# Sixteen column-block sums of a decoder layer's first modulation, in another order and at other places of VectorE's program

## The chip, the cores and the metric

The kernel runs on one core of a Trainium2 chip. The metric is the time of one execution on the device, in microseconds (us). The core has five engines that run their own programs and wait for each other through semaphores: TensorE (PE in the profile, with its weight loads as PEld), VectorE (DVE), ScalarE (ACT), GpSimd (POOL) and SyncE (SP), which here issues most of the transfers from memory.

## The reference

One decoder layer on a sequence of 1024 tokens of width 1024, in float32. A conditioning vector `c` gives six rows of 1024 numbers, the modulation; the first two, shift and scale of the token-mixing part, are what this change deals with. Cut to that:

```python
mod = c_act @ w_ada[l] + b_ada[l]          # c_act = silu(c), w_ada: 1024 x 6144
sh1, sc1, g1, sh2, sc2, g2 = [m[:, None, :] for m in jnp.split(mod, N_MOD, axis=-1)]
h = rmsnorm(x, pre_w_mix[l]) * (1.0 + sc1) + sh1
proj = h @ w_in[l]                         # attention q, k, v and the recurrence's inputs
...
mix = jnp.concatenate([attn, rec], axis=-1) @ w_out[l]
x = x + g1 * rmsnorm(mix, post_w_mix[l])
h = rmsnorm(x, pre_w_mlp[l]) * (1.0 + sc2) + sh2
u = jnp.square(jax.nn.relu(h @ w_up[l]))
x = x + g2 * rmsnorm(u @ w_down[l], post_w_mlp[l])
```

## The kernel before

The program is one long function that lays the layer out in stages: the first modulation together with the first projections (about the first 70 us), attention, the gated recurrence, the output projection, and the channel mixing, which is half of the time. All matrix products are done in split precision: each operand is a rounded part `h` (hi) and a rest `l` (lo), and three products hi x hi, hi x lo, lo x hi are summed.

**The first stage.** Tokens go in groups of four blocks of 128; the width of 1024 goes in eight column blocks `kb` of 128. The loop over `kb` (lines 430 to 485) does for the first 512 tokens:

- `first_evac`: the transposed tokens of block `kb`, `xT` in PSUM, are scaled and shifted by the modulation. ScalarE writes the hi part `hhi`, POOL forms `f` from it, VectorE writes the rest `hlo` from `xT` and `f`.
- `first_mm(kb, tb, 0)`: TensorE multiplies `hhi` by the weights `wq` and `wkv`, hi and lo. These matmuls are `pq` and `pk` in the profile.
- `first_wql`, `first_kv`: VectorE makes the lo parts of the next weights (`wq1l` and so on).
- `first_T`: TensorE transposes the tokens of the next block. There is one PSUM buffer for `xT`, so this waits until `hlo` of the block before has been written.
- `first_mm(kb, tb, 1)`: TensorE multiplies `hlo` by the hi weights.

Shift and scale of a block must be there before its `first_evac`. The modulation's columns are made in four parts, `q`. For the first two parts (columns blocks 0 to 3 of `kb`) TensorE sums over the 1024 inputs itself (`mod_mm`, `mod_copy`, `mod_fold`; tiles `pm` and `ms`). For the last two, `(2, 0)` and `(3, 0)`, VectorE does: `mod_sum` takes eight weight tiles of 128 x 512, multiplies each by a column of `cs` and adds it to `macc1`; `mod_turn` has TensorE transpose the sum (`pmt`), VectorE reduces it (`mred`) and four short operations make the shift `sh1` and the scale `a1`. Part `(2, 0)` serves the column blocks 4 and 5, part `(3, 0)` the blocks 6 and 7, so `mod_turn` stands at the ends of `kb` 3 and 5.

**The weight tiles.** `load_wa` loads them from memory, part by part, and within a part in the order `kp` 0 to 3 with `gate` 0 and 1 in turn (lines 353 to 356). `mod_sum`'s index `k` means tile `wa1[q, k % 4, k // 4]`, that is `kp = k % 4` and `gate = k // 4`. So the tiles are loaded in the order k = 0, 4, 1, 5, 2, 6, 3, 7. In the program order below, `wa1_20_3` is gate 1 of part 2 with kp 3, hence k = 7; the last number of a name is a buffer number.

**What sets the order.** The order is written out by hand. Line 360 pins ScalarE, VectorE, POOL and TensorE: from there on each engine runs its instructions in the order in which the code issues them, and an instruction that waits holds back all behind it on its engine. The sync queue issues its loads in the order of the code too.

**The places the change touches** are the calls of `mod_sum`: at line 469, behind `mod_fold` and `mod_turn` of `kb` 2 and 4, for k = 0 to 4, and at line 461, at the head of the second half of `kb` 3 and 5, for k = 5 to 7:

```python
        if kb in (3, 5):
            mod_sum((kb // 2 + 1, 0), range(5, KB))
...
        if kb in (2, 4):
            mod_sum((kb // 2 + 1, 0), range(5))
```

Of the kernel before, what the change touches and what calls it, by code (L numbers as in the profile page):

```python
# [18 lines left out]
KB = D // P  # L19
# [28 lines left out]
def hybrid_layer(ctx: ExitStack, tc: tile.TileContext, I, out, dbg=None):  # L48
# [3 lines left out]
    def pin(on, *engines):  # L52
        for e in engines:
            e.pinned = on
# [31 lines left out]
    def t_(name, shape=(P, 512), dt=F32):  # L86
        return T2.tile(list(shape), dt, tag="t2", name=name)
# [4 lines left out]
    def tp_ps(name):  # L92
        return pb.tile([P, 512], F32, tag="b", name=name)

    def a_ps(name):
        return pa.tile([P, 512], F32, tag="aps", name=name)
# [8 lines left out]
    def load_x(tb, hfs=(0, 1)):  # L105
        for hf in hfs:
            xh[tb][hf] = (m_ if tb < 4 else hT_)(f"x{tb}_{hf}")
            SP.dma_start(xh[tb][hf], I["x"][tb * P:(tb + 1) * P, hf * 512:(hf + 1) * 512])
# [99 lines left out]
    def norm_scale(th, hf, eng, tbs=range(4)):  # L208
        for tb in tbs:
            xt = xh[4 * th + tb][hf]  # L210
            if eng is ACT:
                ACT.activation(xt, xt, AF.Copy, scale=rx[th][:, tb:tb + 1])
            else:
                DVE.tensor_scalar(xt, xt, rx[th][:, tb:tb + 1], None, ALU.mult)

    def first_T(th, kb, mk=tp_ps):
        pst = mk(f"xT{th}_{kb}")
        hf, col = kb // 4, (kb % 4) * P
        for j in range(4):
            PE.transpose(pst[:, j * P:(j + 1) * P], xh[th * 4 + j][hf][:, col:col + P], ident)  # L220
        return pst
# [12 lines left out]
    def first_evac(th, kb, pst, then=None):  # L234
        hh[kb][th] = (hT_(f"hhi{kb}_{th}", F32R), hT_(f"hlo{kb}_{th}", F32R))
        c = slice(kb, kb + 1)
        split_evac(pst, a1[:, c], sh1[:, c], ns1[:, c], *hh[kb][th], f"f{th}_{kb}", then)
# [4 lines left out]
    def load_raw(mk, name, src, eng=None):  # L242
        rw = mk(name)
        (eng or SP).dma_start(rw, src)
        return rw

    def load_split(mk, name, src, eng=None, raw=None):
        hi, lo = mk(name + "h", dt=F32R), mk(name + "l", dt=F32R)
        for c in range(0, src.shape[1], 512):
            rw = load_raw(raw_, f"{name}r{c}", src[:, c:c + 512]) if raw is None else raw  # L250
            hc = hi[:, c:c + 512]
            ACT.activation(hc, rw, AF.Copy)
            (eng or DVE).tensor_tensor(lo[:, c:c + 512], rw, hc.bitcast(F32), ALU.subtract)
        return hi, lo
# [26 lines left out]
    def mod_mm(q, kps=range(4)):  # L281

        n = 256 if q[0] else P
        if kps[0] == 0:
            pm[q] = a_ps(f"pm{q[0]}_{q[1]}")
        for kp in kps:
            for i in range(4):
                w2 = wa1[q, kp, i // 2][:, i % 2 * 256:][:, :256] if q[0] else wa1[q, kp, 0][:, P * i:P * i + P]
                PE.matmul(pm[q][32 * i:32 * i + 32, :n], lhsT=csr[:, 2 * kp + i % 2, :], rhs=w2,
                          start=(kp == 0), stop=(kp == 3), tile_position=(0, 32 * i))  # L290

    def mod_copy(q):
        n = 256 if q[0] else P
        pm[q, 0] = t_(f"ms{q[0]}_{q[1]}", (P, n))
        DVE.tensor_copy(pm[q, 0], pm[q][:, :n])
# [16 lines left out]
    def mod_sum(q, ks):  # L312
        for k in ks:
            wt, c = wa1[q, k % 4, k // 4], cs[:, k:k + 1]
            if k == 0:
                macc1[q] = t_(f"macc1_{q[0]}")
                DVE.tensor_scalar(macc1[q], wt, c, None, ALU.mult)
            else:
                DVE.scalar_tensor_tensor(macc1[q], wt, c, macc1[q], ALU.mult, ALU.add)
# [82 lines left out]
    def first_kv(qt, eng=POOL):  # L402
        hi, lo = load_split(m_, f"wkv{qt}", I["w_kv"][qt], eng=eng, raw=wkvr[qt])
        wkv.extend([(hi[:, 0:256], lo[:, 0:256]), (hi[:, 256:512], lo[:, 256:512])])
# [13 lines left out]
    def first_wq(kb):  # L418
        hi, lo = (g_(f"wq{kb}{n}", dt=F32R) for n in "hl")
        ACT.activation(hi, wqr[kb], AF.Copy)  # L420
        wq.append((hi, lo))

    def first_wql(kb):
        hi, lo = wq[kb]
        DVE.tensor_tensor(lo, wqr[kb], hi.bitcast(F32), ALU.subtract)
# [4 lines left out]
    for kb in range(KB):  # L430
        q = nextq.get(kb)
        first_evac(0, kb, xT0[kb], None if kb else lambda: first_kv(0, DVE))
        if kb == 0:
            pq0 += [tp_ps("pq2"), tp_ps("pq3")]
            pks = [tp_ps("pk01"), tp_ps("pk23")]
            pk0 += [pks[tb // 2][:, tb % 2 * 256:tb % 2 * 256 + 256] for tb in range(4)]
            wkvr.append(load_raw(raw_, "wkvr3", I["w_kv"][3]))
        if kb + 1 < KB:
            first_wq(kb + 1)
        if kb == 3:  # L440
            norm_scale(0, 1, ACT)
            pin(True, SP)
            for hf in range(2):
                for tb in range(4, TB):
                    load_x(tb, (hf,))
            pin(False, SP)
        if kb and q:
            mod_mm(q, range(2))
        for which in ((0,), (1,)) if kb == 0 else ((0, 1),):
            first_mm(kb, 0, 0, which)  # L450
            first_mm(kb, 1, 0, which)
            if kb and q:
                mod_mm(q, range(2, 4))
                mod_copy(q)
            first_mm(kb, 2, 0, which)
            first_mm(kb, 3, 0, which)
            if kb == 0 and which[0] == 0:
                mod_mm(q)
                mod_copy(q)
        if kb in (3, 5):  # L460
            mod_sum((kb // 2 + 1, 0), range(5, KB))
        if kb + 1 < KB:
            first_wql(kb + 1)
        if q:
            mod_fold(q)
        if kb in (3, 5):
            mod_turn((kb // 2 + 1, 0))
        if kb in (2, 4):
            mod_sum((kb // 2 + 1, 0), range(5))
        if kb in (1, 3, 5):  # L470
            first_kv((kb + 1) // 2, DVE)
        if kb + 1 < KB:
            xT0.append(first_T(0, kb + 1))
        if kb in (5, 6):
            for tb in range(4, TB):
                norm_sq(tb, (kb - 5,))
        if kb == 6:
            norm_rstd(1, 0, 4)
            norm_scale(1, 0, DVE)
        if kb == 7:  # L480
            norm_scale(1, 1, DVE)
        if kb == KB - 1:
            xT1 = [first_T(1, 0), first_T(1, 1, a_ps)]
        for tb in range(4):
            first_mm(kb, tb, 1)
# [1290 lines left out]
```

## Time and profile before

| | before |
|---|---|
| median of 3 runs | 1097.88 us (1097.61 to 1098.4) |
| the profiled execution, as a run | 1101.11 us |
| its span, first to last instruction | 1099.3 us |
| instructions | 16110 |
| moved between memory and the core | 203.37 MB, 185 GB/s in the mean |

The profile is of one execution. A busy time is the time in which an engine executed something, a share is that of the span. Rows of a timeline give start and duration in us, the engine, the line, the operation, the tile written, the tiles read, the sizes and the count; in brackets stands the idle time ahead and what ended it. All operations of a pinned engine go through a helper and so carry one line, L39: they are told apart by their tiles. Names are cut there to their letters, so `macc1_2` and `macc1_3` are both `macc`, the two `mod_turn` both `pmt`.

The busy share of VectorE in the 40 slices of the span (27.5 us each, in tenths), with that of TensorE above it, shows where the first stage lies, in the first two to three slices:

```profile
PE   8999999999999999999999999999999999999995
...
DVE  3875777878865574559767767676678787999876
```

### The profile page before, as it was taken

Reading aid. Unit: us, or ns where it says so; the run is one execution under the profiler, and the core shown is the slowest. Engines: PE = TensorE matmul, PEld = TensorE weight load, DVE = VectorE, ACT = ScalarE, POOL = GpSimd, SP = SyncE. Lnnn points to the kernel's source line nnn. Section 1 sums busy time; section 2 is a strip of 40 time slices with the busy share of each in tenths; the row PEclk is TensorE's granted clock in tenths of the full one; section 3 lists DMA queues with packets and bytes.
Section 4 is the critical chain, followed back from the end, with each engine's and each line's share of the span. In section 5 each row is a group of like instructions: output and inputs, shape, how many; then the busy total and the mean of one; then the engine's idle time right before and its main releaser. Section 6 shows DMA issues by size and latency. Waiting matters only on the chain.

```text
span 1099.3 us, 16110 instructions
## 1 busy us (share of the span) xinstructions
PE 1074.6 (98%) x5483; PEld 877.0 (80%) x5483; DVE 802.8 (73%) x1339; ACT 583.6 (53%) x1206; POOL 373.1 (34%) x499
## 2 busy tenths in 40 slices
PE   8999999999999999999999999999999999999995
PEld 6788776788888888888888888888878888888884
DVE  3875777878865574559767767676678787999876
ACT  3445544364565764566655555556575543446434
POOL 1153211043324653432543443434233333330014
PEclk9999999999999999999999999999999999999998
DMA  9701301534310352324577676767799888998637
GB/s 350 257 11 52 122 1 38 185 103 140 124 57 13 105 183 96 125 79 143 191 249 249 229 259 203 260 218 255 267 376 318 274 291 259 341 311 271 187 80 131
DMA packets 101586, 203.37 MB, mean 185 GB/s; under 512 B 13024, under 2 KB 13680, under 8 KB 101504
## 3 DMA queue, kind: packets, MB, share of 16 engines
q1 hardware_dynamic: 85968, 154.52, 41.6%
q0 software_dynamic: 15392, 47.57, 14.6%
q8 instruction: 43, 0.70, 0.3%
q14 instruction: 39, 0.32, 0.1%
q10 hardware_dynamic: 144, 0.26, 0.1%
HBM read 147.25 MB, written 55.05 MB: 184 GB/s over the span
## 4 chain that ended last, share of the span: by engine, by line
PE 83%; DMA 7%; DVE 5%; ACT 2%; issue 1%; POOL 1%; SPq 0%; DVEq 0%; POOLq 0%; ACTq 0%
PE pda L39 14%; PE pua L39 13%; PE pdc L39 7%; PE po L39 7%; PE puc L39 6%; PE pu L39 4%; PE pdb L39 4%; PE phg L39 4%; PE phq L39 3%; PE phf L39 3%; PE pub L39 3%; PE pv L39 3%; PE pq L39 2%; DMA wa<-wada 1%; DMA dwr<-td 1%
## 5 line engine op out<-in xcount | busy, mean ns | idle before, releaser
L39 POOL TENSOR_TENSOR b<-b,b 128x512 f32<-128x512 f32 x64 | 88.8, 1388 | 235.5 <-DMA b<-w_dn 235.2
L39 ACT ACTIVATE dw<-dwr 128x512 fp32r<-128x512 f32 x72 | 45.4, 630 | 48.3 <-DMA dwr<-td 30.9
L39 ACT ACTIVATE s<-s 128x512 f32<-128x512 f32 x84 | 52.9, 631 | 33.3 <-DVE s L39 32.0
L39 DVE TENSOR_TENSOR acc<-pda,acc 128x512 f32<-128x512 f32 x68 | 46.9, 689 | 15.3 <-PE pda L39 14.9
L39 DVE TENSOR_TENSOR dw<-dwr,dw 128x512 fp32r<-128x512 f32 x72 | 53.6, 744 | 5.8 <-ACT dw L39 5.8
L39 POOL DMA_DIRECT2D td<-b x64 | 36.3, 567 | 21.6 <-POOL b L39 18.7
L39 ACT ACTIVATE s<-pua 128x512 f32<-128x512 f32 x28 | 16.7, 597 | 39.5 <-PE pua L39 34.0
L39 ACT ACT_TABLE_LOAD x28 | 35.9, 1283 | 1.2 <-PEq L1769 0.7
L39 POOL TENSOR_TENSOR rrf<-ssf,mhalf 128x1 f32<-128x1 f32 x7 | 7.8, 1252 | 83.9 <-DVE ssf L39 83.9
L39 DVE TENSOR_TENSOR wt<-s,wt 128x512 fp32r<-128x512 f32 x42 | 33.8, 805 | 2.6 <-ACT wt L39 2.5
L39 DVE SCALAR_TENSOR_TENSOR macc<-wada,cs,macc 128x512 f32<-128x512 f32 x42 | 33.4, 795 | 3.0 <-DMA wada<-wada 2.5
L39 POOL DMA_DIRECT2D b<-w_dn x64 | 34.4, 540 | 0.0
L39 POOL TENSOR_TENSOR comb<-comb,rd 128x512 f32<-128x512 f32 x8 | 11.7, 1458 | 63.3 <-DVE rd L39 44.2
L39 PE MATMUL pua<-bt_0h,wt 128*128 128x512 f32 x84 | 32.7, 389 | 0.0
L39 PE MATMUL pua<-bt_1h,wt 128*128 128x512 f32 x84 | 32.7, 389 | 0.0
L39 PE MATMUL pua<-bt_2h,wt 128*128 128x512 f32 x84 | 32.7, 389 | 0.0
L39 PE MATMUL pua<-bt_3h,wt 128*128 128x512 f32 x84 | 32.7, 389 | 0.0
L39 DVE TENSOR_TENSOR wt<-a,wt 128x512 fp32r<-128x512 f32 x42 | 31.6, 753 | 0.9 <-ACT wt L39 0.9
L39 ACT ACTIVATE wt<-s 128x512 fp32r<-128x512 f32 x42 | 26.3, 626 | 8.9 <-DVE s L39 8.7
L39 DVE TENSOR_TENSOR s<-puc,s 128x512 f32<-128x512 f32 x14 | 9.7, 690 | 28.5 <-issue 26.0
L39 PE MATMUL pda<-dw,du_6h 128*128 128x512 f32 x96 | 29.8, 390 | 0.5 <-DVE dw L39 0.5
L39 DVE TENSOR_TENSOR acc<-pdc,acc 128x512 f32<-128x512 f32 x36 | 24.8, 690 | 7.3 <-PE pdc L39 7.1
(763 smaller groups left out, 3775.4 us busy)
## 6 DMA issues: line engine op xcount, KB each, us to landing
dur<-ud SPq DMA_DIRECT2D x112, 256.0 KB, 4.7
wada<-wada SPq DMA_DIRECT2D x64, 256.0 KB, 3.8
b<-w_dn POOLq DMA_DIRECT2D x64, 256.0 KB, 5.4
td<-b POOLq DMA_DIRECT2D x64, 256.0 KB, 3.5
dwr<-td SPq DMA_DIRECT2D x64, 256.0 KB, 4.4
a<-w_u SPq DMA_DIRECT2D x56, 256.0 KB, 4.3
dwr<-w_dn SPq DMA_DIRECT2D x48, 256.0 KB, 4.8
ud<-s SPq DMA_DIRECT2D x42, 256.0 KB, 3.6
```

The costliest lines, as they stand in the source:

```text
L39: ins = op(*args, **kw)
```

## The change

The sixteen calls of `mod_sum` for single tiles are taken in the order in which the tiles are loaded and set at other places of the loop. Within each part the set of tiles is the same; only the order of the additions and the places differ.

```diff
@@ -451,24 +451,33 @@
             if kb and q:
                 mod_mm(q, range(2, 4))
+                mod_sum((2, 0), (0, 4))
                 mod_copy(q)
...
-        if kb in (3, 5):
-            mod_sum((kb // 2 + 1, 0), range(5, KB))
         if kb + 1 < KB:
             first_wql(kb + 1)
+        if kb == 1:
+            mod_sum((2, 0), (1,))
+        if kb == 3:
+            mod_sum((3, 0), (0,))
         if q:
             mod_fold(q)
         if kb in (3, 5):
             mod_turn((kb // 2 + 1, 0))
-        if kb in (2, 4):
-            mod_sum((kb // 2 + 1, 0), range(5))
+        if kb == 2:
+            mod_sum((2, 0), (2, 6, 3, 7))
+        if kb == 4:
+            mod_sum((3, 0), (5, 2, 6, 3, 7))
         if kb in (1, 3, 5):
             first_kv((kb + 1) // 2, DVE)
+        if kb == 1:
+            mod_sum((2, 0), (5,))
+        if kb == 3:
+            mod_sum((3, 0), (4, 1))
```

What that does to VectorE's program, at three places. Each row is one instruction: the line, the operation, the tile written, the tiles read, the size.

**In `kb` 1.** Before, between the rest `hlo1` and the shift and scale of the blocks 2 and 3 (`m1s1`), VectorE's program has the copy of TensorE's partial sums and one weight's lo part:

```order
L39 SCALAR_TENSOR_TENSOR hlo1_0_410<-xT0_1_396,a1_130,f0_1_412 128x512
L39 COPY ms1_0_443<-pm1_0_418 128x256
L39 TENSOR_TENSOR wq2l_416<-wqr2_181,wq2h_415 128x512
L39 TENSOR_TENSOR m1s1_0_456<-pm1_0_418,c_tab_97 128x2
L39 TENSOR_TENSOR sh1_128<-pm1_0_418,c_tab_97 128x2
```

The same place in the changed program:

```order
L39 SCALAR_TENSOR_TENSOR hlo1_0_410<-xT0_1_396,a1_130,f0_1_412 128x512
L39 TENSOR_SCALAR macc1_2_443<-wa0_20_0_187,cs_107 128x512
L39 SCALAR_TENSOR_TENSOR macc1_2_443<-wa1_20_0_189,cs_107,macc1_2_443 128x512
L39 COPY ms1_0_446<-pm1_0_418 128x256
L39 TENSOR_TENSOR wq2l_416<-wqr2_181,wq2h_415 128x512
L39 SCALAR_TENSOR_TENSOR macc1_2_443<-wa0_20_1_191,cs_107,macc1_2_443 128x512
L39 TENSOR_TENSOR m1s1_0_460<-pm1_0_418,c_tab_97 128x2
```

Three sums of the part for the blocks 4 and 5 (k = 0, 4, 1) now stand here, two ahead of the copy and one behind the lo part; the fourth (k = 5) stands a few rows on, ahead of `hlo2`.

**In `kb` 2 and 3.** Before, from the lo part `wq3l` to `mred`, the first operation behind the transposes of the finished sum:

```order
L39 TENSOR_TENSOR wq3l_485<-wqr3_183,wq3h_484 128x512
L39 TENSOR_SCALAR macc1_2_504<-wa0_20_0_187,cs_107 128x512
L39 SCALAR_TENSOR_TENSOR macc1_2_504<-wa0_20_1_191,cs_107,macc1_2_504 128x512
L39 SCALAR_TENSOR_TENSOR macc1_2_504<-wa0_20_2_195,cs_107,macc1_2_504 128x512
L39 SCALAR_TENSOR_TENSOR macc1_2_504<-wa0_20_3_199,cs_107,macc1_2_504 128x512
L39 SCALAR_TENSOR_TENSOR macc1_2_504<-wa1_20_0_189,cs_107,macc1_2_504 128x512
L39 SCALAR_TENSOR_TENSOR hlo3_0_524<-xT0_3_510,a1_130,f0_3_526 128x512
L39 SCALAR_TENSOR_TENSOR macc1_2_504<-wa1_20_1_193,cs_107,macc1_2_504 128x512
L39 SCALAR_TENSOR_TENSOR macc1_2_504<-wa1_20_2_197,cs_107,macc1_2_504 128x512
L39 SCALAR_TENSOR_TENSOR macc1_2_504<-wa1_20_3_201,cs_107,macc1_2_504 128x512
L39 TENSOR_TENSOR wq4l_530<-wqr4_203,wq4h_529 128x512
L39 TENSOR_REDUCE mred1_2_577<-pmt2_572 128x4
```

The same stretch in the changed program:

```order
L39 TENSOR_TENSOR wq3l_490<-wqr3_183,wq3h_489 128x512
L39 SCALAR_TENSOR_TENSOR macc1_2_443<-wa0_20_2_195,cs_107,macc1_2_443 128x512
L39 SCALAR_TENSOR_TENSOR macc1_2_443<-wa1_20_2_197,cs_107,macc1_2_443 128x512
L39 SCALAR_TENSOR_TENSOR macc1_2_443<-wa0_20_3_199,cs_107,macc1_2_443 128x512
L39 SCALAR_TENSOR_TENSOR macc1_2_443<-wa1_20_3_201,cs_107,macc1_2_443 128x512
L39 SCALAR_TENSOR_TENSOR hlo3_0_527<-xT0_3_513,a1_130,f0_3_529 128x512
L39 TENSOR_TENSOR wq4l_533<-wqr4_203,wq4h_532 128x512
L39 TENSOR_SCALAR macc1_3_572<-wa0_30_0_209,cs_107 128x512
L39 TENSOR_REDUCE mred1_2_579<-pmt2_574 128x4
```

Four sums instead of eight are left, all ahead of `hlo3`, and the first of the next part (`macc1_3`, k = 0) has come in ahead of `mred`.

**In `kb` 4 and 5.** Before, the part for the blocks 6 and 7 stands as that for 4 and 5 did: five sums behind `wq5l`, then `hlo5`, then three sums, `wq6l` and the second `mred`. In the changed program, from the lo part `wkv2l` of `kb` 3 on:

```order
L39 TENSOR_TENSOR wkv2l_587<-wkvr2_207,wkv2h_586 128x512
L39 SCALAR_TENSOR_TENSOR macc1_3_572<-wa1_30_0_211,cs_107,macc1_3_572 128x512
L39 SCALAR_TENSOR_TENSOR macc1_3_572<-wa0_30_1_213,cs_107,macc1_3_572 128x512
L39 SCALAR_TENSOR_TENSOR hlo4_0_606<-xT0_4_592,a1_130,f0_4_608 128x512
L39 TENSOR_TENSOR wq5l_612<-wqr5_205,wq5h_611 128x512
L39 SCALAR_TENSOR_TENSOR macc1_3_572<-wa1_30_1_215,cs_107,macc1_3_572 128x512
L39 SCALAR_TENSOR_TENSOR macc1_3_572<-wa0_30_2_217,cs_107,macc1_3_572 128x512
L39 SCALAR_TENSOR_TENSOR macc1_3_572<-wa1_30_2_219,cs_107,macc1_3_572 128x512
L39 SCALAR_TENSOR_TENSOR macc1_3_572<-wa0_30_3_221,cs_107,macc1_3_572 128x512
L39 SCALAR_TENSOR_TENSOR macc1_3_572<-wa1_30_3_223,cs_107,macc1_3_572 128x512
L39 SCALAR_TENSOR_TENSOR hlo5_0_650<-xT0_5_636,a1_130,f0_5_652 128x512
L39 TENSOR_TENSOR wq6l_656<-wqr6_225,wq6h_655 128x512
```

Two sums stand ahead of `hlo4` and five between `wq5l` and `hlo5`; `hlo5` has come to stand behind all of them, with `wq6l` next and then `mred`. The order on the other engines is unchanged.

## The prediction

> **What bounds the kernel now.** First the core's clock and the busy times, to see which engine sets the time. The columns of the second row are busy us, share of the span and instructions.
>
> ```profile
> core 0: 1099.3 us, clock 0.995
> PE 1074.6 (98%) x5483; PEld 877.0 (80%) x5483; DVE 802.8 (73%) x1339; ACT 583.6 (53%) x1206; POOL 373.1 (34%) x499
> ```
>
> TensorE (PE) is busy for 1074.6 of 1099.3 us, so a change that adds and removes no matmul can win at most part of the other 24.7 us. Which part it aims at stands in the view of waits, for TensorE and for its weight loads (PEld): us in total, times, longest.
>
> ```profile
> PE pmt L39 <- DVE macc L39: 2.3, 2, 1.3
> PEld pmt L39 <- DVE macc L39: 2.7, 2, 1.5
> ```
>
> TensorE waits twice, for 2.3 us, until VectorE (DVE) has summed a column block (`macc1`) that the transposes `pmt` read. That is the largest entry of that view. The timeline of TensorE (start, duration, idle before) shows both places and, between them, a transpose group that did not have to wait:
>
> ```profile
> 38.84 0.27 PE L39 MATMUL pk<-wkv1l,hhi 128*128 128x256 f32 x1
> 40.08 0.66 PE L39 MATMUL pmt<-c_tab,macc 128*128 128x128 f32 x4 [0.97 <-DVE macc L39]
> ...
> 42.79 0.50 PE L39 MATMUL pq<-wq4h,hhi 128*128 128x512 f32 x1 [0.20 <-ACT hhi L39]
> ...
> 45.57 0.28 PE L39 MATMUL pk<-wkv2l,hhi 128*128 128x256 f32 x1
> 45.69 0.60 PE L39 MATMUL xT<-c_tab,x 128*128 128x128 f32 x4
> ...
> 50.20 0.28 PE L39 MATMUL pk<-wkv2l,hhi 128*128 128x256 f32 x1
> 51.78 0.66 PE L39 MATMUL pmt<-c_tab,macc 128*128 128x128 f32 x4 [1.29 <-DVE macc L39]
> ...
> 54.48 0.50 PE L39 MATMUL pq<-wq6h,hhi 128*128 128x512 f32 x1 [0.20 <-ACT hhi L39]
> ```
>
> Without a wait, four transposes begin 0.12 us after the matmul ahead of them (45.57 to 45.69) and take 0.60, not 0.66. After each `pmt` the next block's shift and scale go through VectorE and ScalarE, and the first matmul on the new block starts 2.05 us after the end of the transposes (40.74 to 42.79; 52.44 to 54.48). At both places that matmul waits 0.20 us for this chain. So what counts is when `pmt` ends, and not when TensorE's own work between would be done.
>
> Then VectorE, where the sums stand in the way:
>
> ```profile
> 27.90 0.42 DVE L39 COPY ms<-pm 128x256 f32<-128x256 f32 x1 [2.70 <-PE pm L39]
> 28.24 0.68 DVE L39 TENSOR_TENSOR wq2l<-wqr,wq2h 128x512 fp32r<-128x512 f32 x1
> 29.88 0.16 DVE L39 TENSOR_TENSOR m1s<-pm,c_tab 128x2 f32<-128x2 f32 x1 [0.96 <-PE pm L39]
> ...
> 36.07 1.06 DVE L39 SCALAR_TENSOR_TENSOR macc<-wa,cs,macc 128x512 f32<-128x512 f32 x1
> 37.06 0.74 DVE L39 SCALAR_TENSOR_TENSOR hlo<-xT,a,f 128x512 fp32r<-128x512 f32 x1
> 37.72 2.31 DVE L39 SCALAR_TENSOR_TENSOR macc<-wa,cs,macc 128x512 f32<-128x512 f32 x3
> ...
> 43.62 0.75 DVE L39 SCALAR_TENSOR_TENSOR hlo<-xT,a,f 128x512 fp32r<-128x512 f32 x1 [1.07 <-POOL f L39]
> 44.28 0.68 DVE L39 TENSOR_TENSOR wq5l<-wqr,wq5h 128x512 fp32r<-128x512 f32 x1
> ...
> 51.64 0.69 DVE L39 TENSOR_TENSOR wq6l<-wqr,wq6h 128x512 fp32r<-128x512 f32 x1
> 52.47 0.69 DVE L39 TENSOR_REDUCE mred<-pmt 128x4 f32<-128x512 f32 x1
> ```
>
> The three last sums of a block run back to back until 40.03 (37.72 plus 2.31) and, at the second place, until `wq6l` begins at 51.64, and `pmt` follows at once; yet VectorE idled 2.70, 0.96 and 1.07 us shortly before. Three dependent sums take 2.31 us, so one takes about 0.75 and starts 0.78 after the one ahead; an operation that depends on nothing new starts 0.08 before the end of the one ahead (37.06 to 37.72 at 0.74). I use these steps below.
>
> **The change, part by part.** It adds and removes no instruction and no transfer; each queue keeps its own order but VectorE's. Sixteen sums move.
>
> First block (columns 4 and 5 of the modulation), two sums into the 2.70 us ahead of `ms`. They now read weights soon after landing, which is the new wait. The weight loads are issued by the sync queue (SP), the rows being its timeline, a piece of the chain of work, and the landing times of all 32 loads of this kind (min, median, max):
>
> ```profile
> 20.11 5.23 SPq L39 DMA_DIRECT2D wa<-wada x8
> 19.51 5.49 DMA wkvr<-w_kv
> DMA to landing us min/median/max: 4.9/5.2/6.4
> ```
>
> Eight issues in 5.23 us are one per 0.70. The first two tiles, at the median, land at 25.3 and 26.0; the transfer just ahead of them landed at 25.00. The sums are then done by 26.8, and `ms` at 27.90 isn't late. With the longest latency of any of the 32, the second lands at 27.2 and its sum ends at 27.95, which is 0.05 late. The third sum stands behind `wq2l`: 28.24 plus 0.60 plus 0.75 is 29.6, ahead of `m1s` at 29.88. So this costs 0 to 0.05 on VectorE, and nothing on the path. The fourth goes ahead of the next `hlo`, the last four behind `wq3l`: from 33.19, 3 x 0.78 + 0.75 gives 36.3, and with the delays that follow below 37.1. TensorE wants the block at 38.84 + 0.12 = 38.96. The cover is about 1.9 us, and `hlo`, now behind the sums, is done at 37.8, ahead of the transposes that overwrite its source at 39.3. **First term:** `pmt` ends at 38.96 + 0.60 = 39.56 instead of 40.74, a gain of 1.18 us, and the next matmul on new data moves with it, to 41.61.
>
> Second block. Its first sum sits between `wq4l` and `mred`, where VectorE waits for TensorE anyway. Two follow in the 1.07 us ahead of `hlo` at 43.62, which is 42.44 after the shift. From 41.3 (end of the short work behind `mred`) two sums last 1.53 us, more than the gap; `hlo` slips to 42.9, or 43.2 with a delay. TensorE overwrites its source at 45.69 - 1.18 = 44.51, so this is covered by 0.6 us. Then `wq5l` and five sums: 43.2 + 0.66 + 0.60 = 44.5, plus 4 x 0.78 + 0.75 is 48.3, and 48.7 with one more delay. TensorE wants them at 50.20 + 0.12 - 1.18 = 49.14: cover 0.4. **Second term:** `pmt` ends at 49.74 instead of 52.44, in all 2.70 us earlier, the weight loads' figure too. **Third term:** in the old order `hlo` ran among the sums and only `wq6l` stood between the last sum and `mred`; now both do. `hlo` from 48.7 and `wq6l` until 50.0 keep VectorE past 49.78, when `mred` could begin, by 0.16 us or so. That is on the path. The sum is 2.70 - 0.16 = **2.54 us**.
>
> The delays are those of a meeting with POOL's step `f`:
>
> ```profile
> 35.82 0.77 POOL L39 TENSOR_SCALAR f<-hhi,ns 128x512 f32<-128x512 f32 x1 [3.93 <-ACT hhi L39]
> 42.89 0.69 POOL L39 TENSOR_SCALAR f<-hhi,ns 128x512 f32<-128x512 f32 x1 [6.29 <-ACT hhi L39]
> 47.27 1.02 POOL L39 TENSOR_SCALAR f<-hhi,ns 128x512 f32<-128x512 f32 x1 [3.69 <-ACT hhi L39]
> ```
>
> Alone (42.89) `f` takes 0.69. The sum that started at 36.07, inside the `f` of 35.82, took 1.06 instead of 0.75: 0.31 more. The change puts sums beside four `f`, of which two (near 41.7 and 46.1 after the shift) lie in the chain to the second `pmt`. Bounds for each: nothing, if they miss each other, or a whole `f` of 0.69. I take 0.31, since it is this operation's own row. With nothing the gain is 2.70; with 0.69 twice VectorE is 0.76 later than above, `mred` with it, and the gain is 1.8.
>
> The Trainium skill, page "SBUF — State Buffer", section "SBUF: two separate sides", speaks against such a placing: a VectorE operation with two SBUF inputs and a GpSimd operation that reads SBUF hold a shared port by turns, and the later one stands still for the other's whole length. The trace agrees in direction (1.06 against 0.75, 1.02 against 0.69), but in these meetings only part of the other's length was lost. By a full block each time the sum would be the 1.8 above; by the row it is 2.54.
>
> Behind 54.48 all is released by this matmul's block or by buffers that later work frees, so I carry the gain to the end one for one. The profiled execution then goes from 1099.3 us to 1096.8. It took 1101.11 us with what lies around its span; the median of the runs shown, without a profile, is 1097.88. The same 2.54 off gives 1095.3.
>
> **Rivals.**
> (a) *The second wait comes back in part.* Its cover is only 0.4 us, and `hlo` and `wq6l` now queue behind the last sum. With the delays at a full `f` the time is 1097.88 - 1.8 = 1096.1; if the second gain goes wholly, 1097.88 - 1.18 = 1096.7. For it: ten operations in a row on VectorE with no slack but that. Against: both meetings in the old trace cost about 0.3.
> (b) *The change moves what wasn't late.* In the chain of work the sum at 39.28 follows a transfer:
>
> ```profile
> 35.31 3.95 DMA x<-x
> 39.28 0.76 DVE macc L39
> ```
>
> If that landing (39.26) really released the sum, weights and not order set the pace, and the time stays 1097.9. Against: this sum reads weights issued near 25 us, not x, and it is the third of an even group (37.72 plus 2 x 0.78). I take the landing for a coincidence.
> (c) *Slower, by one staged load.* In the channel mixing, weights go through memory and back, and one piece of the chain has no cover:
>
> ```profile
> 792.03 7.16 DMA dwr<-td
> PE pda L39 <- DVE dw L39: 0.5, 1, 0.5
> ```
>
> TensorE already waits 0.5 us there, so a load that is pushed behind one more transfer shows at once. If earlier issue lets POOL's and SP's transfers meet in another order and one such load takes its 7.16 us a second time, the time is 1097.88 - 2.54 + 7.16 = 1102.5; it decides from 2.54 us of added lateness on. Against: both queues wait for computed data, so they move together.
>
> **How the numbers follow.** The forecast, both waits gone at a gain of 1.9 to 2.9 (the bounds, 0.2 us wider above for matmul ends that are modelled), has 0.74: 1095.0 to 1096.0, likeliest 1095.3. (a) has 0.11, (b) 0.06, (c) 0.05, a larger gain 0.04. The range takes in the forecast and (a): 1094.7 to 1097.0. A change of 0.2%, 2.2 us, is about what a measurement of this kernel can tell from none, and the forecast lies just beyond it at 1095.7: some eight tenths of its chance gain more. Faster is 0.74 x 0.8 + 0.04 = 0.63; slower is (c) and some unknown, 0.06; within it 0.31.
>
> **What would show it.** Right: no wait of `pmt` for `macc`; `pmt` ends near 39.6 and 49.7; the two `hhi` waits of 0.20 behind them grow to 0.3 to 0.6, as TensorE arrives sooner than the chain; the matmul of 54.48 starts near 51.9; `ms` stays near 27.9; all later stages stand 2.5 us earlier. Wrong: `ms` or `m1s` late (landing), a wait left at the second `pmt` (a), or a shift that is there at 60 us and gone or reversed behind 760 us (c).

## The result and the profile after

| | before | after |
|---|---|---|
| median of 8 runs each, us | 1097.81 (1096.59 to 1099.34) | 1095.39 (1093.67 to 1097.61) |
| the profiled execution, as a run, us | 1101.11 | 1095.36 |
| its span, us | 1099.3 | 1093.6 |

The ratio is 0.9977, with a 95% interval of 0.9968 to 0.9986: the changed kernel is faster by 1.5 to 3.5 us. The forecast was 1095.3.

The page of the changed kernel, cores and busy times as before, and VectorE's busy share in 40 slices:

```profile
core 0: 1093.6 us, clock 0.996
...
PE 1071.9 (98%) x5483; PEld 875.9 (80%) x5483; DVE 801.2 (73%) x1339; ACT 585.4 (54%) x1206; POOL 373.9 (34%) x499
...
DVE  4866768878865564559767767676777787899876
```

The engines run as many instructions as before. VectorE's first slice has gone from 3 to 4 tenths, but that isn't the change: a second execution of the kernel before (first experiment) has 4 there too, and its first stage, like that of the changed kernel, began 2 us sooner in the span than in the first profile of before. The view of waits between 24 and 60 us, the same columns as before, shows what became of TensorE's two waits:

```profile
DVE macc L39 <- DMA wa<-wada: 2.7, 2, 2.4
...
DVE mred L39 <- PE pmt L39: 0.8, 1, 0.8
...
PE pq L39 <- ACT hhi L39: 0.4, 2, 0.2
```

There is no row of `pmt` for `macc` left. VectorE now waits for the landing of weights (`wa`), and once for TensorE's transposes (`mred` for `pmt`), where before TensorE waited for VectorE. TensorE's timeline at the two places:

```profile
37.30 0.28 PE L39 MATMUL pk<-wkv1l,hhi 128*128 128x256 f32 x1
37.42 0.60 PE L39 MATMUL pmt<-c_tab,macc 128*128 128x128 f32 x4
...
40.06 0.50 PE L39 MATMUL pq<-wq4h,hhi 128*128 128x512 f32 x1 [0.20 <-ACT hhi L39]
...
47.49 0.28 PE L39 MATMUL pk<-wkv2l,hhi 128*128 128x256 f32 x1
47.61 0.60 PE L39 MATMUL pmt<-c_tab,macc 128*128 128x128 f32 x4
...
50.25 0.50 PE L39 MATMUL pq<-wq6h,hhi 128*128 128x512 f32 x1 [0.20 <-ACT hhi L39]
```

Both `pmt` begin 0.12 us after the matmul ahead and take 0.60, as transposes without a wait do. The time from the end of `pmt` to the first matmul on the new block is as before: 2.04 (38.02 to 40.06, 48.21 to 50.25). VectorE's timeline shows what it has come to:

```profile
25.61 0.49 DVE L39 TENSOR_SCALAR macc<-wa,cs 128x512 f32<-128x512 f32 x1 [2.44 <-DMA wa<-wada]
26.36 0.75 DVE L39 SCALAR_TENSOR_TENSOR macc<-wa,cs,macc 128x512 f32<-128x512 f32 x1 [0.26 <-DMA wa<-wada]
27.03 0.42 DVE L39 COPY ms<-pm 128x256 f32<-128x256 f32 x1
...
32.18 3.42 DVE L39 SCALAR_TENSOR_TENSOR macc<-wa,cs,macc 128x512 f32<-128x512 f32 x4
35.52 0.74 DVE L39 SCALAR_TENSOR_TENSOR hlo<-xT,a,f 128x512 fp32r<-128x512 f32 x1
36.18 0.68 DVE L39 TENSOR_TENSOR wq4l<-wqr,wq4h 128x512 fp32r<-128x512 f32 x1
36.78 0.47 DVE L39 TENSOR_SCALAR macc<-wa,cs 128x512 f32<-128x512 f32 x1
38.06 0.69 DVE L39 TENSOR_REDUCE mred<-pmt 128x4 f32<-128x512 f32 x1 [0.81 <-PE pmt L39]
...
39.74 1.85 DVE L39 SCALAR_TENSOR_TENSOR macc<-wa,cs,macc 128x512 f32<-128x512 f32 x2
41.52 0.74 DVE L39 SCALAR_TENSOR_TENSOR hlo<-xT,a,f 128x512 fp32r<-128x512 f32 x1
...
42.78 4.20 DVE L39 SCALAR_TENSOR_TENSOR macc<-wa,cs,macc 128x512 f32<-128x512 f32 x5
46.89 0.74 DVE L39 SCALAR_TENSOR_TENSOR hlo<-xT,a,f 128x512 fp32r<-128x512 f32 x1
47.55 0.68 DVE L39 TENSOR_TENSOR wq6l<-wqr,wq6h 128x512 fp32r<-128x512 f32 x1
48.25 0.69 DVE L39 TENSOR_REDUCE mred<-pmt 128x4 f32<-128x512 f32 x1
```

Read it from the two `mred`, the first operations that need the transposes. The first waited 0.81 us for TensorE: about that much is to spare at the first block. The second has no idle row: `wq6l` ended at 48.23, `pmt` at 48.21. It is on time, but only just. And at the top the sum of the second tile waited until 26.36, so that `ms` came at 27.03 behind it.

**Which spans to compare.** The two profiled spans differ by 5.7 us, the medians by 2.4. Before's profiled execution is 3.3 us above its own median: its first matmul started at 17.89 us, that of the changed kernel at 15.86, and the second execution of the kernel before at 15.76 with a span of 1095.5. The first profile of before also lost 1.2 us more than that second one between 801 and 889 us, where TensorE waited 0.54 us for `dw`. From here on stages are measured between starts of matmuls, which leaves the start out: A from the first `pq<-wq0h,hhi` to the first `pq<-wq4h,hhi` (the first `pmt` lies in it), B from there to `pq<-wq6h,hhi` (the second `pmt`); L is both and the 4.74 to 4.77 from there to `pq<-wq7h,hhi`. All starts are rows of TensorE's timelines.

| us | first matmul | `ms` after it | A | B | L |
|---|---|---|---|---|---|
| before | 17.89 | 10.01 | 24.90 | 11.69 | 41.33 |
| before, second execution | 15.76 | 10.01 | 24.90 | 11.70 | 41.34 |
| after | 15.86 | 11.17 | 24.20 | 10.19 | 39.13 |
| first part only | 15.88 | 11.19 | 24.23 | 11.69 | 40.69 |
| second part only | 15.64 | 10.03 | 25.07 | 10.16 | 39.97 |
| tiles in the order 0 to 7 | 15.68 | 12.22 | 25.27 | 10.18 | 40.20 |
| one sum ahead of `ms` | 15.61 | 10.40 | 23.73 | 10.18 | 38.65 |
| the same, `pmt` earlier | 16.17 | 10.76 | 23.46 | 10.09 | 38.32 |
| two more sums, first block | 16.34 | 11.81 | 25.39 | 10.19 | 40.33 |
| one more sum, second block | 15.97 | 11.72 | 24.77 | 10.81 | 40.35 |

B repeats within 0.03 us between programs that agree in that part, and A did in the two executions of the kernel before, where no sum stands ahead of `ms`. So A fell by 0.70 and B by 1.51: 2.21 in all (L shows 2.20 to 2.21). With two sums ahead of `ms`, A differs from one execution to the next: "first part only" and "one more sum, second block" have the same first block as the changed kernel, and A is 24.23 and 24.77 there. With the latter, the gain would have been 1.6. The gain isn't given back: against the second execution of before, and with a first matmul that was 0.10 later, the changed kernel's first `pua` matmul comes 2.15 us earlier (508.06 against 510.21), its first `pdc` matmul 2.14 (785.50 against 787.64) and its last matmul 2.14 (1080.12 against 1082.26). The span is 1.9 shorter.

### The profile page after: what moved, and what is told of

Its sections match the earlier page's. It is cut to its first block, busy times and chain, and to the rows that moved or that the text cites. A ratio compares the mean times of both kernels' runs of the same rounds, so it can differ in the third digit from the quotient of the medians.

```text
span 1093.6 us, 16105 instructions
## 1 busy us (share of the span) xinstructions
PE 1071.9 (98%) x5483; PEld 875.9 (80%) x5483; DVE 801.2 (73%) x1339; ACT 585.4 (54%) x1206; POOL 373.9 (34%) x499
## 4 chain that ended last, share of the span: by engine, by line
PE 90%; DVE 3%; DMA 2%; ACT 2%; POOL 1%; issue 1%; SPq 0%; DVEq 0%; POOLq 0%; ACTq 0%
PE pda L39 16%; PE pua L39 14%; PE pdc L39 8%; PE po L39 8%; PE puc L39 7%; PE phg L39 4%; PE pu L39 4%; PE pdb L39 4%; PE phq L39 3%; PE pub L39 3%; PE phf L39 3%; PE pq L39 3%; PE pv L39 3%; PE pk L39 2%; PE o L39 1%; DMA wa<-wada 1%
## 5 line engine op out<-in xcount | busy, mean ns | idle before, releaser
L39 DVE TENSOR_TENSOR wt<-s,wt 128x512 fp32r<-128x512 f32 x42 | 36.9, 878 | 2.2 <-ACT wt L39 2.1
```

Source lines behind the costliest of these rows:

```text
L39: ins = op(*args, **kw)
```

## The experiments

Diffs are against the changed kernel unless said otherwise; ratios are against the kernel before. These runs were made on three chips, and on each the kernel before ran beside them, with medians of 1097.88 to 1097.92 us. In the expectations "waits" is the theory of the prediction (TensorE's two waits for the sums set the end), and "landing" the one that weights not yet landed take part of the gain.

### The kernel before, once more

No edit: it gives a second profile of the kernel before.

> The kernel before, unchanged, for a second profile of it. The first-stage interval (from the first matmul pq<-wq0h,hhi to the first pq<-wq7h,hhi) was 41.33 us before (17.89 to 59.22) and 39.13 in the changed kernel (15.86 to 54.99). Theory 'waits': this interval is set by the order of VectorE's work and comes out at 41.3 again, with the two waits of pmt at 1.0 and 1.3; the rest of the 5.7 us between the two profiled spans (start of the first matmul 2.03 us sooner, about 1.2 us near 800 us) is chance of the executions and will differ here; time 1097.8, ratio 1.000 within 0.001. Rival 'luck': the two waits depend on when the loads landed in that execution, and the interval is nearer to 40.

1098.34 us (11 runs; ratio 1.0, 0.9991 to 1.0009), span 1095.5. Its waits between 24 and 60 us:

```profile
DVE ms L39 <- PE pm L39: 2.7, 1, 2.7
...
PE pmt L39 <- DVE macc L39: 2.3, 2, 1.3
```

The two waits are those of the first profile, so they belong to the program and not to one execution. What differs is the start. The sync queue's issues of the tiles in question began at 20.11 in the first profile of before, 2.22 us after the first matmul. In this second execution and in the changed kernel they began at about the same time of the span, but 3.83 and 3.85 us after the first matmul:

```profile
19.59 5.92 SPq L39 DMA_DIRECT2D wa<-wada  x8
```

```profile
19.71 5.59 SPq L39 DMA_DIRECT2D wa<-wada  x8
```

In the table's other executions it was 3.80 to 4.00 us. The first profile of before is the odd one out.

### One part of the change at a time

First part only: the sums for `(3, 0)` go back to their old order and places.

```diff
+        if kb == 5:
+            mod_sum((3, 0), range(5, KB))
...
-        if kb == 3:
-            mod_sum((3, 0), (0,))
...
-            mod_sum((3, 0), (5, 2, 6, 3, 7))
+            mod_sum((3, 0), range(5))
...
-        if kb == 3:
-            mod_sum((3, 0), (4, 1))
```

> Only the first block's eight sums (part 2, for the column blocks 4 and 5) stand as in the changed kernel; the second block's stand as before. Theory 'waits': the first pmt wait goes (gain 1.18), the second stays at 1.3 us; the two sums ahead of ms cost 0.4 to 0.5 by waiting for their tiles, as in the changed kernel's trace. Interval 41.33 - 1.18 + 0.49 = 40.6, time about 1097.1. Rival 'the waits are one': the lateness that the first wait shows is only handed on, the second pmt wait grows to about 2.3 and the interval stays at 41.3, 1097.8.

1096.83 us (11 runs), ratio 0.9989 (0.998 to 0.9998). L is 40.69. A is that of the changed kernel, B that of before, and one wait of `pmt` for `macc`, of 1.3 us, is left.

Second part only: the sums for `(2, 0)` go back.

```diff
-                mod_sum((2, 0), (0, 4))
...
+        if kb == 3:
+            mod_sum((2, 0), range(5, KB))
...
-        if kb == 1:
-            mod_sum((2, 0), (1,))
...
-            mod_sum((2, 0), (2, 6, 3, 7))
+            mod_sum((2, 0), range(5))
...
-        if kb == 1:
-            mod_sum((2, 0), (5,))
```

> Only the second block's eight sums (part 3, for the column blocks 6 and 7) stand as in the changed kernel; the first block's stand as before. Theory 'waits': the first wait of pmt stays at 1.0, the second goes (gain 1.5); nothing waits for landing ahead of ms. But the second block's first sum now stands ahead of mred when mred is late, which costs 0.3 to 0.4 there. Interval 41.33 - 1.5 + 0.35 = 40.2, time about 1096.7. Rival 'the waits are one': without the first block's move nothing is won, 41.3 and 1097.8.

1096.24 us (11 runs), ratio 0.9982 (0.9973 to 0.9991). L is 39.97, A 25.07, B 10.16. A is 0.17 above that of before: the first sum of `(3, 0)` stands ahead of `mred`, and here, where the first `pmt` is late, it is in its way; the `hhi` wait behind is 0.36 instead of 0.20.

The two parts alone bring 0.65 and 1.37; with the 0.17 that only the second one alone pays they make 2.19, and both together bring 2.21. So the two waits are separate: each is worth its own time, whatever becomes of the other.

### The places of the change, with the tiles in the order 0 to 7

```diff
-                mod_sum((2, 0), (0, 4))
+                mod_sum((2, 0), (0, 1))
...
-            mod_sum((2, 0), (1,))
+            mod_sum((2, 0), (2,))
...
-            mod_sum((2, 0), (2, 6, 3, 7))
+            mod_sum((2, 0), (4, 5, 6, 7))
...
-            mod_sum((3, 0), (5, 2, 6, 3, 7))
+            mod_sum((3, 0), (3, 4, 5, 6, 7))
...
-            mod_sum((2, 0), (5,))
+            mod_sum((2, 0), (3,))
...
-            mod_sum((3, 0), (4, 1))
+            mod_sum((3, 0), (1, 2))
```

> The places of the changed kernel, but within each block the tiles are summed in the order 0 to 7 instead of the order of loading 0, 4, 1, 5, 2, 6, 3, 7. Theory 'landing': the second sum ahead of ms needs the third tile loaded, which lands 0.65 us after the second, so ms starts about 0.65 us later than in the changed kernel (27.03 at a first matmul at 15.86) and the matmuls behind m1s with it; interval 39.13 + 0.6 = 39.7, time about 1096.0. Rival 'places only': the order of the tiles costs nothing, 39.1 and 1095.4.

1096.05 us (11 runs), ratio 0.998 (0.9971 to 0.9989). VectorE's timeline, and behind it TensorE's row of the waits:

```profile
25.84 0.49 DVE L39 TENSOR_SCALAR macc<-wa,cs 128x512 f32<-128x512 f32 x1 [2.84 <-DMA wa<-wada]
27.23 0.75 DVE L39 SCALAR_TENSOR_TENSOR macc<-wa,cs,macc 128x512 f32<-128x512 f32 x1 [0.91 <-DMA wa<-wada]
27.90 0.42 DVE L39 COPY ms<-pm 128x256 f32<-128x256 f32 x1
```

```profile
PE pm L39 <- DVE ms L39: 1.2, 1, 1.2
```

The second sum takes the third tile loaded, waits 0.91 us for it, and the copy `ms` behind it holds TensorE for 1.2 us. A is 25.27, above that of before: the first block's gain is gone, and a wait for weights has taken the place of the wait for sums. B, whose tiles have long landed, keeps its whole gain (10.18). "Landing" held in kind, and L is 0.5 above the expectation. Of the 1.05 us by which `ms` is later here than in the changed kernel, counted from the first matmul, the order explains the 0.65 more that the second sum waits (0.91 against 0.26), as expected. The other 0.4 is not the order: the first tile, which is the same in both, also came 0.41 us later in this execution (its sum began 10.16 after the first matmul, against 9.75). So the order of loading matters at one spot only, ahead of `ms`.

### One sum ahead of the copy instead of two

```diff
-                mod_sum((2, 0), (0, 4))
+                mod_sum((2, 0), (0,))
...
-            mod_sum((2, 0), (1,))
+            mod_sum((2, 0), (4,))
...
-            mod_sum((2, 0), (2, 6, 3, 7))
+            mod_sum((2, 0), (5, 2, 6, 3, 7))
...
-            mod_sum((2, 0), (5,))
+            mod_sum((2, 0), (1,))
```

> The changed kernel with only one sum (k = 0) ahead of ms instead of two; the others move up one place each (k = 4 behind wq2l, k = 1 ahead of hlo2, then 5, 2, 6, 3, 7 behind wq3l). Theory 'landing': in the changed kernel ms and m1s came late behind the second sum, which waited for its tile until 26.36, and TensorE lost 0.49 us by the first matmul on block 2; with one sum, done at about 26.1, this is won back and five sums still end before pmt. Interval 39.13 - 0.49 = 38.65, time about 1094.9. Rival 'more sums in a row': five behind wq3l make pmt or mred late, 39.1 or more, 1095.4.

1094.74 us (7 runs), ratio 0.9972 (0.9961 to 0.9982), with the kernel before at 1097.88 (12 runs) on that chip. VectorE's timeline:

```profile
25.61 0.49 DVE L39 TENSOR_SCALAR macc<-wa,cs 128x512 f32<-128x512 f32 x1 [2.66 <-DMA wa<-wada]
26.01 0.42 DVE L39 COPY ms<-pm 128x256 f32<-128x256 f32 x1
```

The copy no longer stands behind the second tile. A is 23.73, 1.17 below that of before, where the first term of the prediction was 1.18; L is 38.65, the expected one. What the changed kernel loses in A, 0.47 us, is this landing. The column `ms` of the table shows from where a landing costs anything: here `ms` is 0.39 later than in the kernel before and in the next experiment 0.75, both for nothing, while 1.16 in the changed kernel cost 0.47. The transposes that need `ms` show why, in the changed kernel and then here:

```profile
27.50 0.71 PE L39 MATMUL pm<-sel,ms 128*128 128x128 f32 x4
```

```profile
26.98 0.61 PE L39 MATMUL pm<-sel,ms 128*128 128x128 f32 x4
```

In the kernel before, they began 1.33 us after `ms` (27.90, 29.23), in the changed one 0.47 (27.03, 27.50): 0.86 of lateness is hidden by TensorE's other work. Counted from the first matmul, they start 0.27 later in the changed kernel than here (11.64 against 11.37); they also take 0.1 longer, and the first matmul on the next block is held up by another 0.1. As a whole time the step from the changed kernel to this one lies within the intervals of both; L shows it.

### The first transposes four matmuls earlier

The kernel of the experiment before, with the transposes of the first sum ahead of the last group of `first_mm` in `kb` 3 (the function `mod_turn` split in two), the first sum of `(3, 0)` behind `mod_turn`, and in `kb` 5 the lo part `wq6l` behind it too.

```diff
             first_mm(kb, 2, 0, which)
+            if kb == 3:
+                mod_flip((2, 0))
             first_mm(kb, 3, 0, which)
...
-        if kb + 1 < KB:
+        if kb + 1 < KB and kb != 5:
             first_wql(kb + 1)
...
-        if kb == 3:
-            mod_sum((3, 0), (0,))
...
             mod_turn((kb // 2 + 1, 0))
+        if kb == 5:
+            first_wql(6)
+        if kb == 3:
+            mod_sum((3, 0), (0,))
```

> As e4, and the first pmt stands four matmuls earlier in TensorE's program (ahead of the last token block's hhi matmuls of kb 3); on VectorE the second block's first sum goes behind mred's group, and in kb 5 wq6l goes behind it too. Theory 'chain': behind pmt the chain over mred, a1 and hhi is late by 0.20 idle, 0.36 from start to start; 0.7 us sooner it is hidden. Interval 38.65 - 0.36 = 38.3, time about 1094.5. Rival 'VectorE is full': with VectorE's work squeezed between the two pmt the second one waits for its sums by 0.3 or more, and the interval stays at 38.6.

1094.67 us (6 runs), ratio 0.997 (0.9959 to 0.9982). L is 38.32, and the view of waits has no row of `pq` for `hhi` any more. At the first place the wait is gone, because TensorE has other work between the transposes and the block that needs them: A is 0.27 shorter than in the experiment before. At the second place, where only `wq6l` moved, nothing is won: the matmul still starts 2.04 us after the end of `pmt` (47.68 to 49.72), and TensorE still idles 0.13 us ahead of it, too short for the view to list. B is 0.09 shorter, which it had gained before `pmt`. All this is too little to be seen in the time of the whole. It is the fastest of the versions run, level with the one before it.

### How much room is left: sums that add zero

These put sums with the factor zero behind the real ones, so that VectorE is longer at work ahead of a `pmt`. In the first two, the factor was read from a new tile of 128 x 8.

```diff
+    mzero = tiny0.tile([P, 8], F32, tag="mzero", name="mzero")
+    nc.vector.memset(mzero, 0.0)
...
             mod_sum((2, 0), (2, 6, 3, 7))
+            mod_zero((2, 0), 2)
```

> The changed kernel with two more sums in the first block, behind its last one, that add zero times a tile (the output stays the same). In the changed kernel the sums end at 35.60 and pmt starts at 37.42, so 1.57 us more would be hidden by the prediction's cover of 1.9. Theory 'mred is next': between the last sum and mred stand hlo3, wq4l and the next block's first sum, and VectorE waited only 0.81 us there; so mred is late by 1.57 - 0.81 = 0.76, and the interval is 39.9, time 1096.1. Rival 'cover': 39.1, 1095.4.

and one in the second block instead:

```diff
             mod_sum((3, 0), (5, 2, 6, 3, 7))
+            mod_zero((3, 0), 1)
```

> The changed kernel with one more sum in the second block that adds zero times a tile. There pmt started at 47.61 with the sums done at 46.98, but mred at 48.25 followed wq6l (47.55, 0.68) with no idle time. Theory 'mred is next': all of its 0.78 us is lost, interval 39.9, time 1096.2. Rival 'cover': pmt alone counts and 0.6 us of it is hidden, interval 39.3, time 1095.6.

1114.43 and 1113.77 us (4 runs each; ratios 1.0153 and 1.0147). No theory had this: 16 us above the kernel before, and 18 to 19 above the changed one, for two instructions or one. L was 41.13 and 40.43, so nearly all of the loss lies behind the first stage. It comes from the new tile, not from the sums, as the following runs show; as measures of the room left the two don't serve. The same sums with the factor as a constant, and no new tile:

```diff
+    def mod_zero(q, n):
+        for _ in range(n):
+            DVE.scalar_tensor_tensor(macc1[q], wa1[q, 0, 0], 0.0, macc1[q], ALU.mult, ALU.add)
...
             mod_sum((2, 0), (2, 6, 3, 7))
+            mod_zero((2, 0), 2)
```

> The changed kernel with two more sums in the first block that add a constant zero times a tile, without the extra tile of e5 (the output stays the same). In e5, hidden under slower matmuls everywhere, mred followed the next block's first sum without idle time. From pm<-sel (four matmuls on sel) to the first pq<-wq4h the changed kernel took 40.06 - 27.50 = 12.56 us. Theory 'mred is next': 12.56 + 1.57 - 0.81 = 13.3, and the time 1095.4 + 0.75 = 1096.1 (more if the tiles land late). Rival 'cover of 1.9': 12.56 and 1095.4. Theory 'e5's 16 us came from its extra tile': nothing like 1114 here; rival 'they came from the sums': 1114 again.

1096.27 us (10 runs), ratio 0.9986 (0.9976 to 0.9996). VectorE's timeline:

```profile
36.75 1.42 DVE L39 SCALAR_TENSOR_TENSOR macc<-wa,macc 128x512 f32<-128x512 f32 x2
...
39.34 0.48 DVE L39 TENSOR_SCALAR macc<-wa,cs 128x512 f32<-128x512 f32 x1
39.74 0.68 DVE L39 TENSOR_REDUCE mred<-pmt 128x4 f32<-128x512 f32 x1
```

The `mred` has lost its idle time and follows the sums at once, and `hhi` is late by 0.72 instead of 0.20. From the first `pm<-sel` transposes, which begin as soon as `ms` is written, to `pq<-wq4h,hhi` it takes 13.10 us instead of 12.56: 0.54 is lost. Against the same transposes the sum ahead of `mred` starts 1.43 later than in the changed kernel (39.34 less 28.63, 36.78 less 27.50), so 0.89 was free, the idle 0.81 and the 0.08 by which an operation may begin before the end of the one ahead. The rest of the larger A is `ms`, which was later by 0.64 in this execution. So the room at the first block is 0.9, not the 1.9 by which the sums are ahead of `pmt`: `hlo`, `wq4l` and a sum of the next part stand between.

And one zero sum in the second block:

```diff
             mod_sum((3, 0), (5, 2, 6, 3, 7))
+            mod_zero((3, 0), 1)
```

> The changed kernel with one more sum in the second block that adds a constant zero times a tile, without the extra tile of e6. From the first pq<-wq4h to the first pq<-wq6h the changed kernel took 50.25 - 40.06 = 10.19 us. Theory 'mred is next': 10.19 + 0.7 to 0.78 = 10.9 to 11.0, time 1096.1. Rival 'cover': pmt alone waits, for about 0.2; 10.4 and 1095.6.

1095.65 us (10 runs), ratio 0.9983 (0.9974 to 0.9992). B is 10.81 instead of 10.19, so 0.62 is lost. Counted from `pq<-wq4h,hhi`, `hlo` starts 0.73 later (48.30 less 40.74, 46.89 less 40.06): only 0.1 of it was free. VectorE's timeline, up to the second `mred`, which now starts well behind the end of `pmt` (48.44 plus 0.65):

```profile
47.69 0.69 DVE L39 SCALAR_TENSOR_TENSOR macc<-wa,macc 128x512 f32<-128x512 f32 x1
48.30 0.74 DVE L39 SCALAR_TENSOR_TENSOR hlo<-xT,a,f 128x512 fp32r<-128x512 f32 x1
48.96 0.68 DVE L39 TENSOR_TENSOR wq6l<-wqr,wq6h 128x512 fp32r<-128x512 f32 x1
49.56 0.68 DVE L39 TENSOR_REDUCE mred<-pmt 128x4 f32<-128x512 f32 x1
```

The median of this kernel is not clearly above that of the changed one, though its L is 1.2 longer: half of that is a landing that was late in the profiled execution, itself one of the longer ones at 1097.3, and the runs of both kernels scatter over 3 to 4 us. For steps of half a microsecond the intervals within one execution tell more than whole times.

### What the new tile did

The changed kernel with an unused tile of 32 bytes in each partition, then of 64, set to zero once.

```diff
     mhalf = tiny0.tile([P, 8], F32, tag="mhalf", name="mhalf")
     nc.vector.memset(mhalf, -0.5)
+    pad = tiny0.tile([P, 8], F32, tag="pad", name="pad")
+    nc.vector.memset(pad, 0.0)
```

> The changed kernel with one unused tile of 8 numbers (32 bytes a partition) in the small left-hand pool, written once at the start, so that the large tiles behind it lie 32 bytes further on. Theory 'place in memory': this alone makes the matmuls slower by 1 to 2% and the time 1112 to 1114, as in e5 and e6, with the first stage's waits as in the changed kernel. Rival: the sums or the early write did it another way, and this stays at 1095.4.

```diff
+    pad = tiny0.tile([P, 16], F32, tag="pad", name="pad")
+    nc.vector.memset(pad, 0.0)
```

> The same with a tile of 16 numbers (64 bytes a partition). Theory 'place in memory, in steps of 64 bytes': at 64 bytes the matmuls run as in the changed kernel, 1095.4. Rival 'any shift': slower as with 32 bytes, 1112 to 1114.

1112.59 and 1105.79 us (4 runs each), ratios 1.0136 (1.012 to 1.0151) and 1.0075 (1.006 to 1.009). So a tile that nothing reads costs 17 and 10 us against the changed kernel. The two runs differ in nothing but its size, and by 7 us in time, so it is the room that the tile takes and not the added instruction. That this room moves other tiles in memory is what the code suggests; no view here shows addresses. The busy times by stretches for the changed kernel, then with 32 bytes and with 64; columns: window, its length, TensorE's busy time and instructions, then those of the weight loads, VectorE, ScalarE and POOL, the granted clock, the share of DMA time, GB/s:

```profile
500.00:700.00 200.00, 200.00 (x884) 165.62 (x883) 146.37 (x202) 112.54 (x196) 86.31 (x99) 1.00 0.69 227
800.00:1000.00 200.00, 200.00 (x884) 165.61 (x883) 168.70 (x245) 99.82 (x166) 61.28 (x72) 1.00 0.88 293
```

```profile
500.00:700.00 200.00, 200.00 (x866) 162.47 (x866) 149.32 (x201) 111.85 (x193) 82.59 (x99) 1.00 0.68 224
800.00:1000.00 200.00, 200.00 (x864) 162.24 (x863) 162.36 (x237) 101.33 (x170) 60.41 (x72) 1.00 0.89 298
```

```profile
500.00:700.00 200.00, 200.00 (x877) 164.55 (x876) 144.55 (x201) 113.73 (x197) 81.37 (x95) 1.00 0.68 224
800.00:1000.00 200.00, 200.00 (x864) 161.75 (x863) 165.64 (x236) 98.77 (x165) 63.62 (x76) 1.00 0.88 295
```

TensorE is busy all of the time at a granted clock of 1.00 in all three, and with the tile it gets through fewer matmuls. The difference is in the duration of one; the group of `pua` matmuls in the changed kernel and with 32 bytes (busy us, mean ns):

```profile
L39 PE MATMUL pua<-bt_0h,wt 128*128 128x512 f32 x84 | 32.7, 389 | 0.0
```

```profile
L39 PE MATMUL pua<-bt_0h,wt 128*128 128x512 f32 x84 | 33.2, 395 | 0.0
```

With 64 bytes the stretch from 500 to 700 us lost 7 of 884 and the later one 20, as many as with 32. A theory in steps of 64 bytes fell with that, and so did its rival, that any shift costs the same. Which tile's place matters, and why, is left open.

## Why the prediction was right, and where it was off

**Both waits go, each for its own time.** Right. Neither `pmt` waits; the parts alone show that the waits add up. The two terms were 1.18 for the first and 1.52 more for the second. The second measured 1.51 (B). The first measures 1.17 where nothing else intervenes (one sum ahead of `ms`), but only 0.70 in the changed kernel.

**Landing, "0 to 0.05 on VectorE, and nothing on the path".** This is the step that failed in size: it cost 0.47 on the path in the profiled execution, and about 1.0 in the one with an A of 24.77. The landing times of 25.3 and 26.0 held within 0.4 us (sums at 25.61 and 26.36), and the second sum ends at 27.11, where I had 26.8, but that is luck: the issues began 0.40 sooner than in the profile of before, and the first sum began 5.90 us after them, where I had taken 5.2. What was wrong most is the time at which `ms` is wanted. I took 27.90 from the first profile of before, whose first matmul stands 1.5 to 2.3 us later than in the table's other executions, while the issues of its loads at 20.11 do not (19.45 to 20.14 in the table's others); in the second execution of the kernel before, `ms` started at 25.77. So the sign "`ms` stays near 27.9" can't be read in the time of the span: 27.03 looks early and is 1.16 us late, counted from the first matmul. In that count the sums were done at 11.25 instead of 8.91. Of these 2.34 us, 1.63 are the distance from the first matmul to the issues (3.85 instead of 2.22) and 0.7 the time from issue to sum. By this working either alone would have been hidden: `ms` is wanted at 10.01, and 0.86 of lateness costs nothing. In the table's seven executions with a sum ahead of `ms`, that sum began, with the landing, 9.75 to 10.37 us after the first matmul, so the changed kernel's 9.75 is the earliest of them.

**Third term, 0.16 for `hlo` and `wq6l` ahead of `mred`.** It came out as nothing: `wq6l` ended 0.02 after `pmt`. The zero sum shows that the place itself was rightly named: there is 0.1 us of room, where I had 0.16 too little. So a term that adds ten durations in a row was off by a quarter of a microsecond, and the rival (a) was that near. With the landing's 0.47 against it, the sum of 2.54 became 2.21 in L; the measured gain of 2.4 in the medians, 1.5 to 3.5 by its interval, can't tell the two apart. That 1095.39 came out 0.1 from the forecast is luck to that extent. One figure on the way doesn't follow from its own terms: 37.1 for the end of the first block's last four sums adds 0.8 to 36.3, more than two delays of 0.31. Nothing hung on it: these sums end at 35.60, and `pmt` starts 1.82 later, where I had about 1.9 of cover.

**The delays beside POOL's `f`, 0.31 each.** Right where the sum used it. Four sums took 3.42, two took 1.85 and five took 4.20, against 3.09, 1.53 and 3.87 by the steps without a meeting: 0.33, 0.32 and 0.33 more. The `f` in question lengthened as well:

```profile
40.10 0.96 POOL L39 TENSOR_SCALAR f<-hhi,ns 128x512 f32<-128x512 f32 x1 [5.04 <-ACT hhi L39]
44.55 1.10 POOL L39 TENSOR_SCALAR f<-hhi,ns 128x512 f32<-128x512 f32 x1 [3.50 <-ACT hhi L39]
50.35 0.69 POOL L39 TENSOR_SCALAR f<-hhi,ns 128x512 f32<-128x512 f32 x1 [4.70 <-ACT hhi L39]
```

The last of them met no sum and took 0.69. It isn't the price of every meeting: the sum at 29.57 took its usual 0.75, though an `f` of 0.89 began at 29.99 beside it. By the full block of the Trainium skill, page "SBUF — State Buffer", section "SBUF: two separate sides", each meeting would have cost the later one up to 0.69; no meeting here cost a sum more than 0.33.

**"The two `hhi` waits of 0.20 grow to 0.3 to 0.6."** Wrong: both stayed at 0.20. TensorE doesn't arrive sooner, for `pmt` and the matmuls behind it stand on the same queue: the chain to `hhi` and TensorE's own work both start at the end of `pmt`, 2.04 us before the matmul, whenever that end is. In the runs the wait grows only where VectorE is late for `mred` (0.72 with two zero sums), and goes where other work stands between (the earlier transposes). The sum didn't use this step.

**The rivals.** (a), the second wait back in part, didn't happen. (b), a change that moves what isn't late, fell with the rows of waits and B; the landing at 39.26 was a coincidence. (c), a staged load that is pushed, didn't show: the lead over the second execution of before is 2.15 us at the first `pua`, still 2.15 at 883 us (`pdc<-dw,du_3h`, 883.42 against 885.57), behind the place in question, and 2.14 at the last matmul. The 0.5 us that TensorE waited for `dw` in the first profile of before is in neither of these two executions.

## What to carry to other kernels

Work moved into an idle stretch of an engine has to be checked at both ends: what it needs (a landing) and what stands behind it on the same engine (here `ms` and `mred`); the room is the least idle time ahead of any of these, not that of the operation that waited before. Take the distance between a load and the compute that needs it from several executions: here one profile had 2.22 us where the others had 3.80 to 4.00. When whole times can't tell two versions apart, intervals between two instructions of the same execution can, to some hundredths of a microsecond.

## What the hardware showed that I had not expected

- **A tile that nothing reads can slow the matmuls.** One of 32 bytes a partition lengthened the mean `pua` matmul from 389 to 395 ns and the kernel by 17 us, one of 64 bytes the kernel by 10. That other tiles came to lie elsewhere in memory is the likely reason, not shown. An experiment that adds even a tiny tile needs a run with the tile alone beside it.
- **Loads slide against compute from one execution to the next.** In the table's executions the issues of the tiles began 3.80 to 4.00 us after the first matmul, but 2.22 in one of the two executions of the kernel before. And from the first of these issues to the first sum it took 5.90 to 6.57 us in the seven executions with a sum ahead of `ms`.
